# Blocks of a triangular inverse on the partitions in another order, with their transfers on other queues

## The chip, the core and the metric

The kernel runs on one core of a Trainium2 chip. The metric is device time in microseconds, the median of several executions. A core has five engines with a queue of instructions each, run in order: TensorE (PE in the profile, its weight loads PEld), VectorE (DVE), ScalarE (ACT), GpSimd (POOL) and SyncE (SP). SyncE computes nothing and issues transfers; ScalarE and GpSimd can issue transfers too. Transfers run on 16 DMA engines that all queues share.

## The reference, cut to what matters

One decoder layer on 512 tokens of width 1024: feed-forward, mixer, feed-forward, norm. The mixer has two branches. The change lies in the second, a gated delta rule with 16 value heads in 8 pairs (a pair shares its query and key head). For every chunk of tokens it needs the inverse `T` of a unit lower triangular matrix:

```python
A = jnp.where(strict, jnp.einsum('bhntk,bhnsk->bhnts', kb, k) * Lmat, 0.0)
T = lax.linalg.triangular_solve(eye + A, jnp.broadcast_to(eye, A.shape),
                                left_side=True, lower=True, unit_diagonal=True)
u = jnp.matmul(T, v * beta[..., None])
w = jnp.matmul(T, kb * jnp.exp(gam)[..., None])
```

Then a recurrence over the chunks uses the inverse. The kernel works with chunks of 128 tokens, so a head has four matrices of 128 x 128 and a pair has eight.

## The kernel before, in words

Dense products are made of weight slabs. `slab` loads 128 x 512 numbers into `raw` (three buffers, on SP's queue), ScalarE rounds them into `whi`, VectorE puts the rest into `wlo` (five buffers of each), and TensorE does three matmuls for every block (L101 to L103). A slab of four blocks is twelve matmuls of 512 columns; slabs for products laid out by tokens (`natural`, weights `wn`) feed matmuls of 256 columns instead.

The program first runs a feed-forward stage, then the mixer, then the second feed-forward stage. In the mixer the string `ORDER` lists steps in program order. `n` (g_n) builds the matrices of one pair and starts the inverse; `i` (g_inv) finishes it; `r` (g_rec) is one chunk of the recurrence, given a high priority; the rest (`q k v z t y`) are dense products that also serve as work beside the recurrences. From this program the framework builds one fixed order for each engine, by a timeline that it simulates at build time. So an edit in one place can move instructions of all engines.

Step `n` makes Gram products on TensorE (L589), loads two decay rows `gb` (gam_rows, L635), and forms `n2`, eight negated triangular matrices. Each has four diagonal blocks of 32 x 32, so a pair has 32 such blocks. They are inverted on GpSimd by substitution, with one column of the result after the other updated by rank-one steps; to spread this over 128 partitions, each block's 32 result columns are split into four groups of eight. The steps:

- `nb`: four stores (SP, L614) put the blocks into DRAM, by b, the place on the diagonal, and s, the matrix.
- `m` (called `gfs` in the profile): four loads bring all 32 blocks to 32 partitions each, once for each column group g. Partition is g, then b, then s (POOL, L617).
- `t` (`ft`): the start values, an identity, from a constant in DRAM (POOL, L619).
- 62 instructions on POOL, two for each of 31 columns (L623, L624).
- `nt`: one store of `t` into DRAM (POOL, L625).
- `tq` (`x` in the profile, from `nt`): sixteen loads of 8 KB, one for each b and g (SP, L629), which put block rows on the partitions.
- `tp`: VectorE copies `tq` into the right column order (L631).

Step `i` then transposes the blocks (VectorE, L658) and joins blocks of 32 to 64 and to 128 by matmuls (L669, L675). The output `yh` of the first branch's projection (y_h) is evicted by ScalarE (L766) and stored into `md` on ScalarE's queue (L767).

Of the kernel before, what the change touches and what calls it, by code (L numbers as in the profile page):

```python
# [8 lines left out]
F32 = mybir.dt.float32  # L9
# [7 lines left out]
P = 128  # L17
T = 512
NT = T // P
# [245 lines left out]
def mixer(tc, mp, e):  # L265
    nc = tc.nc
    pe, act, dve, pool, sp = nc.tensor, nc.scalar, nc.vector, nc.gpsimd, nc.sync
    cs, ident, tri, strict, hm, ones, mhalf = (e[k] for k in ("cs", "ident", "tri", "strict", "hm", "ones", "mhalf"))
    uh, ul, rbc, rcol, rhalf, h = (e[k] for k in ("uh", "ul", "rbc", "rcol", "rhalf", "h"))
    psc, dr, dense, slab, mm3, ux, hd, dbg = (  # L270
        e[k] for k in ("psc", "dr", "dense", "slab", "mm3", "ux", "hd", "dbg"))
    wt, wn, wab, wbh, wbg, wo, dta, psd = (e[k] for k in ("wt", "wn", "wab", "wbh", "wbg", "wo", "dtab", "psd"))

    def ps(name, lane="d"):
        return psc.tile([P, T], F32, tag="p" + lane, name=name, bufs=LANES[lane])

    def v3(ap, a):
        return ap.rearrange("p (a b) -> p a b", a=a)

    def bc(ap, n):  # L280

        return ap.unsqueeze(2).to_broadcast([ap.shape[0], ap.shape[1], n])
# [14 lines left out]
    for size, names in ((1024, "n2:2 gz:2 fs:1 ut:1"), (512, "kn:3 gm:1 qm:2 gb:2 ln:1 at:4 vb:4 t64:2 on:2"),  # L297
                        (256, "ft:1 tp:1 thg:2 x:1 we:1 s:3 w:1"), (128, "fm:1"), (64, "sm:3")):
        for it in names.split():
            n, b = it.split(":")  # L300
# [3 lines left out]
    eye4 = e["hmask"][:, 5:9].rearrange("p a (i c) -> p (a i) c", c=8)  # L304
# [56 lines left out]
    gtd = dr.tile([16, T], F32, name="gtd")  # L361
# [173 lines left out]
    md = dr.tile([KD, P, T], F32, name="md")  # L535
# [25 lines left out]
    def g_n(u, st):  # L561
        kq = st["kq"] = G["kq"][u % 4]
        kn = st["kn"] = G["kn"][u % 4]
        sm = st["sm"] = places["sm"]("sm", (P, 8, 8))
        for i in range(2):
            pt = ps("ptk", "e")
            for c in range(NT):
                pe.transpose(pt[:, c * P:(c + 1) * P], kq[:, c, i], ident)
            if i == 0:
                act.copy(kn, v3(pt, NT))  # L570
            for c in range(NT):
                pc = pt[:, c * P:(c + 1) * P]
                act.activation(pc, pc, AF.Square, accum_out=sm[:, 0, 4 * i + c:4 * i + c + 1])

        hs = slice(2 * u, 2 * u + 2)
        rk = sm[:, 1, 0:4]
        dve.tensor_scalar(rk, sm[:, 0, 0:4], 4.0 * EPS, None, op0=ALU.add)
        pool.tensor_tensor(rk, rk, mhalf[:, :4], op=ALU.pow)
        s8 = lambda i: v3(sm[:, i], NT)
        c2, c3, c1 = st["c2"], st["c3"], st["c1"] = s8(2), s8(3), s8(4)  # L580
        dve.scalar_tensor_tensor(c2, beta[:, :, hs], 1.0, bc(rk, 2), op0=ALU.mult, op1=ALU.mult)
        dve.scalar_tensor_tensor(c3, c2, -1.0, bc(rk, 2), op0=ALU.mult, op1=ALU.mult)
        dve.tensor_tensor(c1, c3, eg[:, :, hs], op=ALU.mult)
        dve.tensor_scalar(c2, c2, 0.5, None, op0=ALU.mult)
        gm, qm = places["gm"]("gm", (P, NT, P)), G["qm"]
        for hf in range(2):
            pq = ps("pgq", "e")
            for c in (2 * hf, 2 * hf + 1):
                pe.matmul(pq[:, (c % 2) * 256:(c % 2) * 256 + 256], kq[:, c, 0],  # L589
                          kq[:, c].rearrange("p a b -> p (a b)"), start=True, stop=True)  # L590
            p4 = pq.rearrange("p (c a b) -> p c a b", c=2, a=2)
            dve.tensor_tensor(gm[:, 2 * hf:2 * hf + 2], p4[:, :, 0], mid(strict, 2), op=ALU.mult)
            dve.tensor_tensor(qm[:, 2 * hf:2 * hf + 2], p4[:, :, 1], mid(tri, 2), op=ALU.mult)
        st["at"] = []
        n2 = st["n2"] = G["n2"][u % 2]
        for i in range(2):
            hd_ = 2 * u + i
            gb = gam_rows(hd_)

            a = G["at"][u % 4][i]  # L600
            for c in range(NT):
                act.activation(a[:, c], gb[:, c], AF.Abs, bias=gam[:, c, hd_:hd_ + 1], scale=-1.0)
            act.activation(a, a, AF.Exp, scale=-1.0)
            for c in range(NT):
                dve.scalar_tensor_tensor(n2[:, i, c], gm[:, c], c3[:, c, i:i + 1], a[:, c], op0=ALU.mult, op1=ALU.mult)
            dve.tensor_tensor(a, qm, a, op=ALU.mult)
            st["at"].append(a)


        nb = dr.tile([4, 8, 32, 32], F32, name=f"nb{u}")  # L610
        nt = dr.tile([4, 4, 8, 32, 8], F32, name=f"nt{u}")
        for b in range(4):
            r = slice(32 * b, 32 * b + 32)
            sp.dma_start(nb[b].rearrange("s i j -> i s j"), n2[r, :, :, r].rearrange("p a c j -> p (a c) j"))  # L614
        m = G["m"]
        for g in range(4):
            pool.dma_start(m[32 * g:32 * g + 32], nb.rearrange("b s i j -> (b s) i j"))  # L617
        t = places["ft"]("ft", (P, 32, 8))
        pool.dma_start(t, eye4)  # L619
        for j in range(31):  # L620
            n, w = 31 - j, j // 4 + 1
            tv = v3(places["fm"]("fm", (P, 96))[:, :n * w], n)
            pool.tensor_tensor(tv, bc(m[:, j + 1:, j], w), t[:, j:j + 1, :w].to_broadcast([P, n, w]), op=ALU.mult)  # L623
            pool.tensor_tensor(t[:, j + 1:, :w], t[:, j + 1:, :w], tv, op=ALU.add)  # L624
        pool.dma_start(nt.rearrange("g b s i c -> (g b s) i c"), t)  # L625
        tq = G["tq"]
        for b in range(4):
            for g in range(4):
                sp.dma_start(tq[32 * b:32 * b + 32, :, g], nt[g, b].rearrange("s i c -> i s c"))  # L629
        tp = st["tp"] = G["tp"][u % 2]  # L630
        dve.tensor_copy(tp.rearrange("p s (c g) -> p s c g", g=4), tq.rearrange("p s g c -> p s c g"))  # L631

    def gam_rows(hd_):
        gb = places["gb"]("gb", (P, NT, P))
        pool.dma_start(gb, gtd[hd_:hd_ + 1].rearrange("o (c b) -> o c b", c=NT).to_broadcast([P, NT, P]))  # L635
        return gb

    def g_v(j, st):
# [123 lines left out]
    def y_h(d):  # L762
        g = ta("yh")
        pt = dense(wbh[d], HH, lambda k: o_h[k])
        with tc.high_priority():
            act.copy(g, pt)  # L766
        act.dma_start(md[d], g)  # L767


    o_h = [None] * HH  # L770
    G = {"kq": [hv[:, i].rearrange("p (c a b) -> p c a b", c=NT, a=2) for i in range(3)]}
# [4 lines left out]
    ex = lambda i, *shape: op[i](f"x{i}", shape)  # L776
    tb, big, col = (P, NT, P), (P, 2, NT, P), (P, 256)

    def room():
        G["kn"] = [pl("kn", tb) for _ in range(3)]  # L780
        G["qm"] = pl("qm", tb)
        G["late"] = pl("qm", tb)
        G["n2"] = [pl("n2", big) for _ in range(2)]
        G["gz"] = [pl("gz", (P, NT, 256)) for _ in range(2)]
        G["at"] = [[pl("at", tb) for _ in range(2)] for _ in range(2)]
        G["vb"] = [[pl("vb", tb) for _ in range(2)] for _ in range(2)]
        G["ut"] = [pl("ut", (P, 8, P)), hv[:, 3].rearrange("p (s b) -> p s b", s=8)]
        G["t64"] = [pl("t64", (64, 8, 64)) for _ in range(2)]
        G["m"] = pl("fs", (P, 32, 32))
        G["tq"] = G["gz"][1].rearrange("p c (a b) -> p (c a b)", b=32).rearrange("p (s g c) -> p s g c", s=8, g=4)  # L790
        for n in ("x", "we", "w"):
            G[n] = [pl(n, col)]
        G["tp"] = [pl("tp", (P, 8, 32))]
        for z in (*G["ut"], *G["t64"]):
            pool.memset(z, 0.0)

    def more():
        G["kq"].append(ex(0, P, NT, 2, P))
        G["gz"].append(ex(1, P, NT, 256))
        for n, i in (("at", 2), ("vb", 3)):  # L800
            e_ = ex(i, *big)
            G[n].append([e_[:, 0], e_[:, 1]])
        e_ = ex(4, *big)
        G["kn"].append(e_[:, 0])
        G["at"].append([G["late"], e_[:, 1]])
        G["ut"].append(ex(5, P, 8, P))
        pool.memset(G["ut"][2], 0.0)
        G["tq"] = ex(6, P, 8, 4, 8)
        e_ = ex(7, P, 4, 256)
        for i, n in enumerate(("x", "we", "w")):  # L810
            G[n].append(e_[:, i])
        G["tp"].append(e_[:, 3].rearrange("p (a b) -> p a b", a=8))
# [33 lines left out]
    for i in range(VH):  # L846
        if i < 8:
            a, b = uh[:, i], ul[:, i]
        elif i < 14:
            ab = places[("n2", "n2", "gz", "gz", "fs", "ut")[i - 8]]("sop", (P, 2, T), F32R)  # L850
            a, b = ab[:, 0], ab[:, 1]
        else:
            a, b = (places[n]("so" + n, dt=F32R) for n in (("on", "on"), ("gm", "ln"))[i - 14])
# [6 lines left out]
    for d in range(8):  # L860
        mi, tg, g = (places[n]("m" + n) for n in ("kn", "vb", "at"))
# [4 lines left out]
        pt = dense(wbg[d], VH, lambda k: so[k], lane=MERGE[d])  # L866
# [5 lines left out]
        a, b = ab[:, 0], ab[:, 1]  # L872
# [3 lines left out]
    for d in range(8):  # L876
        hr = ta("hr")
        sp.dma_start(hr, hd[d])
        pt = dense(wo[d], KD, lambda k: ms[k])
# [21 lines left out]
def layout(i):  # L901
    f = {k: np.asarray(v) for k, v in i.items()}
# [8 lines left out]
    a = np.arange(P)  # L911
    sqc = np.stack([np.eye(P), a[:, None] <= a[None, :], a[None, :] < a[:, None]], 1)
    hmask = np.zeros((P, 9, 64))
    for l, hh in enumerate(LEVELS):
        g, b = np.divmod(np.arange(64), hh)
        hmask[:, l] = (a[:, None] >= 2 * hh * g) & (a[:, None] < 2 * hh * g + hh)
    eye4 = np.eye(32).reshape(32, 8, 4).transpose(2, 0, 1)
    hmask[:, 5:] = np.repeat(eye4, 32, axis=0).reshape(P, 4, 64)
    w_in = f["w_in"][0]
    off = np.cumsum([0, 1024, 1024, 1024, 1024, 1024, 1024, 2048, 16, 16, 2048, 1024, 1024])  # L920
    part = [w_in[:, off[j]:off[j + 1]] for j in range(12)]
# [34 lines left out]
```

## Time and profile before

| what | us |
|---|---|
| median of 3 runs | 1764.5 (1762.9 to 1766.72) |
| the profiled execution | 1758.87 |
| its span, first to last instruction | 1757.1 |
| TensorE busy | 1694.4 (96%) |
| VectorE, ScalarE, GpSimd busy | 954.5, 695.7, 340.6 |

The mean clock granted to TensorE is 0.983. The first feed-forward stage lasts until about 400 us, the pairs' inverses and recurrences lie between about 690 and 1270 us, the second feed-forward stage begins after 1350 us. In the profile a row of a timeline is start, duration, engine, line, operation, output and input; a bracket at its end tells how long the engine had been idle before it and whom it waited for. Rows of waits are: engine, instruction, what it waited for, then total time, count and longest. Tiles share buffers, and the profile names a buffer by one of its users, so `tq` and `tp` appear as `x` or `gtp`, the target of the transposes as `h`, `gut` or `x`.

### The profile page before, as it was taken

How to read it: one execution, taken by the hardware profiler on the slowest of the kernel's cores; microseconds unless marked ns; L12 is line 12 of the kernel's file. 1: busy time of each engine (PE TensorE's matmuls, PEld its weight loads, DVE VectorE, ACT ScalarE, POOL GpSimd, SP SyncE). 2: the span in 40 equal slices, each digit the busy share in tenths (PEclk: the TensorE clock that was granted, in tenths of full speed). 3: DMA queues.
4: the chain of work that ended last, by engine and by line, in shares of the span. 5: the costliest groups of instructions: out<-in, count | busy, mean ns of one | idle time of the engine just before them, and what ended most of it. 6: DMA issues, size and time to landing. Idle time of an engine off the chain costs nothing. (4 is left out here: it accounts for less than half of the span.)

```text
span 1757.1 us, 26109 instructions
## 1 busy us (share of the span) xinstructions
PE 1694.4 (96%) x9362; PEld 1430.0 (81%) x9362; DVE 954.5 (54%) x1968; ACT 695.7 (40%) x1525; POOL 340.6 (19%) x717
## 2 busy tenths in 40 slices
PE   7999999999999999899999999998899999999997
PEld 5888888889889997778878878886688888888886
DVE  4544443335675675455776776665564444444323
ACT  4433333332343334454454555444433433333332
POOL 2000000001121222770336435452000100000001
PEclk9999999999999999899999999998999999999998
DMA  4233233332221223442333343345463333323333
GB/s 154 90 96 96 97 95 110 112 116 66 73 75 53 61 84 115 144 123 55 106 102 100 100 114 93 104 117 156 144 186 114 109 98 99 97 96 93 99 94 108
DMA packets 141922, 182.17 MB, mean 104 GB/s; under 512 B 54992, under 2 KB 59600, under 8 KB 141792
## 3 DMA queue, kind: packets, MB, share of 16 engines
q1 hardware_dynamic: 132448, 159.52, 30.6%
q0 software_dynamic: 3584, 10.49, 2.1%
q10 hardware_dynamic: 5760, 10.49, 1.7%
q8 instruction: 74, 1.21, 0.3%
q14 instruction: 56, 0.46, 0.1%
HBM read 163.64 MB, written 16.81 MB: 103 GB/s over the span
## 5 line engine op out<-in xcount | busy, mean ns | idle before, releaser
L96 ACT CAST whi<-raw 128x512 fp32r<-128x512 f32 (+1 forms) x535 | 328.0, 614 | 643.0 <-PE pmm L102 541.3
L97 DVE TENSOR_TENSOR wlo<-raw,whi 128x512 fp32r<-128x512 f32 (+1 forms) x535 | 371.2, 695 | 368.0 <-ACT whi L96 365.1
L101 PE MATMUL pmm<-uh,whi 128*128 128x512 f32 x1288 | 514.3, 400 | 10.6 <-ACT whi L96 6.3
L102 PE MATMUL pmm<-ul,whi 128*128 128x512 f32 x1288 | 511.8, 397 | 1.9 <-DVE ul L128 1.7
L103 PE MATMUL pmm<-uh,wlo 128*128 128x512 f32 x1288 | 510.0, 396 | 0.0
L101 PEld LDWEIGHTS pmm<-uh,whi 128*128 128x128 f32 x1288 | 244.8, 190 | 63.3 <-ACT whi L96 6.5
L102 PEld LDWEIGHTS pmm<-ul,whi 128*128 128x128 f32 x1288 | 244.6, 190 | 55.3 <-DVE ul L128 6.0
L103 PEld LDWEIGHTS pmm<-uh,wlo 128*128 128x128 f32 x1288 | 244.3, 190 | 50.7 <-DVE wlo L97 0.2
L101 PE MATMUL pnat<-whi,uh 128*128 128x256 f32 x512 | 149.6, 294 | 1.1 <-DVE ggz L327 1.0
L102 PE MATMUL pnat<-wlo,uh 128*128 128x256 f32 x512 | 147.8, 290 | 0.0
L103 PE MATMUL pnat<-whi,ul 128*128 128x256 f32 x512 | 147.8, 290 | 0.0
L101 PE MATMUL pmm<-gh,whi 128*128 128x512 f32 (+1 forms) x374 | 141.0, 377 | 0.0
L103 PE MATMUL pmm<-gh,wlo 128*128 128x512 f32 (+1 forms) x374 | 140.9, 377 | 0.0
L102 PE MATMUL pmm<-gl,whi 128*128 128x512 f32 (+1 forms) x374 | 140.8, 377 | 0.0
L139 POOL TENSOR_TENSOR acc<-acc,sqt 128x512 f32<-128x512 f32 x24 | 32.7, 1363 | 526.3 <-ACT sqt L137 526.0
L101 PEld LDWEIGHTS pnat<-whi,uh 128*128 128x128 f32 x512 | 98.7, 193 | 2.8 <-DVE ggz L327 1.4
L102 PEld LDWEIGHTS pnat<-wlo,uh 128*128 128x128 f32 x512 | 99.0, 194 | 0.8
L623 POOL TENSOR_TENSOR fm<-gfs,ft 128x60 f32<-128x60 f32 (+24 forms) x248 | 91.3, 368 | 42.5 <-DMA gfs<-nb 17.8
L103 PEld LDWEIGHTS pnat<-whi,ul 128*128 128x128 f32 x512 | 98.5, 193 | 0.5
L624 POOL TENSOR_TENSOR ft<-ft,fm 128x60 f32<-128x60 f32 (+24 forms) x248 | 90.4, 365 | 18.9
L101 PEld LDWEIGHTS pmm<-gh,whi 128*128 128x128 f32 x374 | 70.4, 188 | 13.0
L103 PEld LDWEIGHTS pmm<-gh,wlo 128*128 128x128 f32 x374 | 70.4, 188 | 12.9
(345 smaller groups left out, 2115.7 us busy)
## 6 DMA issues: line engine op xcount, KB each, us to landing
raw<-wt SPq DMA_DIRECT2D x128, 256.0 KB, 2.8
raw<-w1a SPq DMA_DIRECT2D x88, 256.0 KB, 2.6
raw<-w1b SPq DMA_DIRECT2D x88, 256.0 KB, 2.6
raw<-wn SPq DMA_DIRECT2D x64, 256.0 KB, 3.1
raw<-w2b SPq DMA_DIRECT2D x45, 256.0 KB, 2.6
raw<-w2a SPq DMA_DIRECT2D x40, 256.0 KB, 2.6
raw<-wbg SPq DMA_DIRECT2D x32, 256.0 KB, 3.3
raw<-wbh SPq DMA_DIRECT2D x16, 256.0 KB, 2.8
```

Source lines behind the costliest of these rows:

```text
L96: act.copy(hi[:, :f], raw[:, :f])
L97: dve.tensor_tensor(lo[:, :f], raw[:, :f], hi[:, :f].bitcast(F32), op=ALU.subtract)
L101: pe.matmul(pt, ah, bh, start=first, stop=False)
L102: pe.matmul(pt, ah, bl, start=False, stop=False)
L103: pe.matmul(pt, al, bh, start=False, stop=last)
L139: pool.tensor_tensor(acc, acc, s, op=ALU.add)
L623: pool.tensor_tensor(tv, bc(m[:, j + 1:, j], w), t[:, j:j + 1, :w].to_broadcast([P, n, w]), op=ALU.mult)
L624: pool.tensor_tensor(t[:, j + 1:, :w], t[:, j + 1:, :w], tv, op=ALU.add)
```

## The change

The partition of a block is now b, then g, then s, instead of g, then b, then s. So each of the four `m` loads takes the eight blocks of one b and repeats them for the four groups, by a source with a leading dimension of four and step zero; and `tq` is loaded by four transfers of 32 KB, one for each b, instead of sixteen of 8 KB. The constant that holds the start values is reordered to match, and the copy into `tp` reads other strides. The `m` and `t` loads and the `nt` store move from GpSimd's queue to SP's; the decay rows `gb` move from GpSimd's queue to ScalarE's; the eviction of `yh` moves from ScalarE to VectorE and the store into `md` from ScalarE's queue to SP's. In the changed kernel the lines from the load of `t` (L619, then L620) to the store `nt` (L625, then L626) have a number higher by one; the others keep theirs.

```diff
-        nt = dr.tile([4, 4, 8, 32, 8], F32, name=f"nt{u}")
+        nt = dr.tile([4, 32, 32, 8], F32, name=f"nt{u}")
...
-        for g in range(4):
-            pool.dma_start(m[32 * g:32 * g + 32], nb.rearrange("b s i j -> (b s) i j"))
+        for b in range(4):
+            sp.dma_start(m[32 * b:32 * b + 32].rearrange("p i j -> p (i j)"),
+                         nb[b].rearrange("s i j -> s (i j)").unsqueeze(0).to_broadcast([4, 8, 1024]))
         t = places["ft"]("ft", (P, 32, 8))
-        pool.dma_start(t, eye4)
+        sp.dma_start(t, eye4)
...
-        pool.dma_start(nt.rearrange("g b s i c -> (g b s) i c"), t)
+        sp.dma_start(nt.rearrange("b q i c -> (b q) i c"), t)
         tq = G["tq"]
         for b in range(4):
-            for g in range(4):
-                sp.dma_start(tq[32 * b:32 * b + 32, :, g], nt[g, b].rearrange("s i c -> i s c"))
+            sp.dma_start(tq[32 * b:32 * b + 32], nt[b].rearrange("q i c -> i q c"))
         tp = st["tp"] = G["tp"][u % 2]
-        dve.tensor_copy(tp.rearrange("p s (c g) -> p s c g", g=4), tq.rearrange("p s g c -> p s c g"))
+        dve.tensor_copy(tp.rearrange("p s (c g) -> p s c g", g=4), tq.rearrange("p (g s) c -> p s c g", g=4))
...
-        pool.dma_start(gb, gtd[hd_:hd_ + 1].rearrange("o (c b) -> o c b", c=NT).to_broadcast([P, NT, P]))
+        act.dma_start(gb, gtd[hd_:hd_ + 1].rearrange("o (c b) -> o c b", c=NT).to_broadcast([P, NT, P]))
...
         with tc.high_priority():
-            act.copy(g, pt)
-        act.dma_start(md[d], g)
+            dve.tensor_copy(g, pt)
+        sp.dma_start(md[d], g)
...
-        G["tq"] = G["gz"][1].rearrange("p c (a b) -> p (c a b)", b=32).rearrange("p (s g c) -> p s g c", s=8, g=4)
+        G["tq"] = G["gz"][1].rearrange("p c (q b) -> p (c q) b", b=8)[:, :32]
...
-        G["tq"] = ex(6, P, 8, 4, 8)
+        G["tq"] = ex(6, P, 32, 8)
...
-    hmask[:, 5:] = np.repeat(eye4, 32, axis=0).reshape(P, 4, 64)
+    hmask[:, 5:] = np.tile(np.repeat(eye4, 8, axis=0), (4, 1, 1)).reshape(P, 4, 64)
```

## The prediction

> **What bounds the kernel now.** I read the page's busy table first, then stretches of time, then who waits on TensorE, then the path of one inverse in the timeline.
>
> ```profile
> PE 1694.4 (96%) x9362; PEld 1430.0 (81%) x9362; DVE 954.5 (54%) x1968; ACT 695.7 (40%) x1525; POOL 340.6 (19%) x717
> ...
> 100.00:125.00 25.00, 25.00 (x112) 20.68 (x112) 11.94 (x19) 8.61 (x15) 0.00 (x0) 1.00 0.32 102
> 675.00:1275.00 600.00, 562.11 (x3568) 472.41 (x3567) 374.61 (x854) 292.52 (x807) 245.66 (x609) 0.96 0.40 113
> 1200.00:1225.00 25.00, 18.30 (x145) 15.14 (x144) 14.53 (x39) 11.77 (x30) 1.66 (x1) 0.80 0.64 184
> 1225.00:1275.00 50.00, 43.62 (x219) 33.50 (x219) 27.50 (x74) 23.64 (x73) 3.27 (x2) 1.00 0.49 149
> ...
> PE pmm L101 <- ACT whi L96: 6.8, 2, 6.3
> PE pq L669 <- DVE h L658: 5.9, 4, 4.1
> PE pus L708 <- DVE x L705: 4.0, 3, 2.6
> PE pq L669 <- DVE gut L658: 2.4, 2, 2.2
> PE pq L675 <- ACT acc L671: 2.0, 1, 2.0
> ```
>
> In a stretch's row the columns are its length, then busy time with instruction counts of PE, PEld, DVE, ACT and POOL, then the granted clock, the DMA share and GB/s. TensorE is the bound: 112 wide matmuls fill 25 us of the first feed-forward stage, 0.223 us each (25 / 112). All that this change can touch lies between 675 and 1275 us, where TensorE is idle 600 - 562.1 = 37.9 us and has a mean clock of 0.96. Waits for the inverse itself (L669, L675) are 5.9 + 2.4 + 2.0 = 10.3 us of it; the other 27.6 us belong to the recurrences, the norms and the transposes. Missing weights are no problem: the wait on `whi` is 6.8 us in all, 6.3 of them one wait at the start.
>
> The path of one inverse, the last (pair 7), from the Gram matmuls (L589) to TensorE's first use (L669):
>
> ```profile
> 1150.02 1.02 PE L589 MATMUL pgq<-x 128*128 128x256 f32 x4
> ...
> 1159.70 1.87 SPq L614 DMA_DIRECT2D nb<-gn  x4
> 1163.30 1.96 POOL L617 DMA_DIRECT2D gfs<-nb  x4 [10.79 <-DMA nb<-gn]
> 1169.21 0.25 POOL L623 TENSOR_TENSOR fm<-gfs,ft 128x31 f32<-128x31 f32 x1 [3.96 <-DMA gfs<-nb]
> ...
> 1199.09 0.61 POOL L625 DMA_DIRECT2D nt<-ft  x1 [0.30 <-POOL ft L624]
> ...
> 1201.12 7.77 SPq L629 DMA_DIRECT2D x<-nt  x16
> 1210.50 0.39 DVE L631 COPY x<-x 128x256 f32<-128x256 f32 x1 [7.08 <-DMA x<-nt]
> 1211.86 0.31 PE L669 MATMUL pq<-h,gn 32*32 32x32 f32 x2 [4.06 <-DVE h L658]
> ...
> 976.85 1.10 PE L589 MATMUL pgq<-h 128*128 128x256 f32 x4 [1.15 <-DVE gqm L593]
> 1034.22 0.24 PE L669 MATMUL pq<-h,gn 32*32 32x32 f32 x2 [1.00 <-DVE h L658]
> ```
>
> The reader is to see that the path is as long as the work that was put beside it: 1211.86 - 1151.04 = 60.8 us in pair 7, 56.3 us in pair 4 (1034.22 - 977.95), and TensorE, which runs its queue in order, reaches L669 4.06 and 1.00 us too early. There is no slack worth the name. So what decides is a difference: how much shorter the path gets, against how much less work the changed order puts beside it.
>
> **What the new order takes away.** TensorE gets the same instructions in both kernels; only their order differs. I counted those between the last L589 and the first L669 of a pair in both orders, mean of pairs 2 to 7. Before: 128.3 matmuls of 512 columns, 103.3 of 256, 80.2 small ones. After: 99.7, 96.0 and 57.3. Priced at 0.223 us, half of that, and 0.13 us (the row below, 1.03 / 8), the loss is 28.6 x 0.223 + 7.3 x 0.112 + 22.9 x 0.13 = 6.4 + 0.8 + 3.0 = 10.2 us for each of six inverses. Pairs 0 and 1 lose about 5 and 7 us and I leave them out: pair 1 keeps 64 us of work beside its path, and pair 0 gains most at `tq`, as its sixteen issues were the slowest.
>
> ```profile
> 1268.27 1.03 PE L749 MATMUL pto<-sq,on 128*128 128x128 f32 x8
> ...
> 1208.99 1.34 SPq L94 DMA_DIRECT2D raw<-wbg  x3
> ...
> 1017.41 0.64 POOL L635 DMA_DIRECT2D gb<-gtd  x1 [0.26 <-ACT x L602]
> 1020.66 0.54 POOL L635 DMA_DIRECT2D gb<-gtd  x1
> ...
> q0 software_dynamic: 3584, 10.49, 2.1%
> ...
> raw<-w1a SPq DMA_DIRECT2D x88, 256.0 KB, 2.6
> ...
> x<-nt SPq DMA_DIRECT2D x128, 8.0 KB, 2.0
> ...
> nb<-gn SPq DMA_DIRECT2D x32, 32.0 KB, 1.7
> ```
>
> **What the path gains, step by step.**
> - *Loading `m`, other issue.* Each of the four loads needs one block `nb[b]` instead of all. The first can go some 0.3 + 1.7 = 2.0 us after the first store's issue (median landing 1.7) instead of 3.6 (1163.30 - 1159.70): 1.6 us gained. From the first issue to the loop took 5.9 us (1169.21 - 1163.30); on SP, with four issues at 0.47 (1.87 / 4) and a landing like a weight slab's 2.6, it would be 1.4 + 2.6 = 4.0: another 1.9. In all 3.5 us, if the transfer itself is as fast as before.
> - *Loading `m`, other shape.* It need not be. Before, each load reads 32 rows of 4 KB. After, the source is 8 rows repeated four times, an outer dimension of 4 with step zero. If a transfer is dealt to the 16 DMA engines along its outer dimension, this one has only four of them. The software queue, which carries these loads now, moved 10.49 MB in 2.1% of 16 engines' 1757.1 us: 590 engine-us, 17.8 GB/s per engine. Four loads of 131,072 bytes take 524,288 / (16 x 17.8) = 1.8 us on 16 engines and 7.4 us on four, 5.5 us more. No row shows a transfer of this shape, so the ends are a gain of 3.5 and a loss of 2.0. I take the loss: the row that gives the gain is for another shape, and the change puts the factor of four in front. On this term the Trainium skill speaks ("DMA: Bandwidth & Descriptors", Rules for kernel authors): the number of engines follows from the slowest dimension that is not of size 1, so a leading zero-step broadcast of c copies confines the whole transfer to at most c engines. By that rule this term is the loss of 2.0 us and the result the forecast; by the rows of the old shape it is the gain, and the result lies near the rival "even" below. No run so far shows which.
> - *The loop on POOL.* Two `gb` issues fall into some loops (0.64 + 0.54 us); they go to ScalarE's queue. 0 to 1.2 gained, 0.6 taken. The 62 instructions stay.
> - *`nt` on SP.* From POOL's issue to SP's first read took 2.0 us (1199.09 to 1201.12). From SP it should be the same; but SP must have reached it, and a weight slab ahead of it waits for up to 12 x 0.223 = 2.7 us. 0 to 2.7 lost, 0 taken: the wait table below has SP there early.
> - *`tq`: 4 loads for 16.* 16 issues took 7.77 us, 0.49 each for 256 pieces of 32 B; three slabs of 128 rows took 1.34, 0.45 each. Twice the pieces cost 0.04 more, so 1024 pieces cost some 0.49 + 6 x 0.04 = 0.73, the last of four issued 2.2 us after the first instead of 7.3. Landing may add 0.4. 4.7 us gained; the ends are 5.8 (pitch unchanged) and 0 (pitch proportional to pieces).
> - *`yh` and `md`.* Eight evictions leave ScalarE (579 ns below) for VectorE, 8 x 0.6 = 4.6 us between 718 and 759 us, and eight `md` issues of 0.33 go behind weight loads on SP. VectorE is 54% busy, SP's 96 saved `tq` issues are worth 43 us (96 x 0.449), so both are taken as nothing. With the cover gone they would cost those 4.6 us once.
> - *`gb` on ScalarE*: 16 issues at 0.33 like `md` now, 5.3 us on an engine that loses 8 x 0.58 + 8 x 0.33 = 7.2. Nothing. The reload of `t` stands right behind a pair's `tq` loads, well ahead of the next pair's `nb`: nothing.
>
> ```profile
> L766 ACT COPY yh<-pmm x8: 577/579/588, 718.3 to 753.7; 128x512 f32<-128x512 f32 x8
> L767 ACTq DMA_DIRECT2D md<-yh x8: 326/327/327, 718.9 to 758.9; - x8
> ...
> L629 SPq DMA_DIRECT2D x<-nt x128: 302/449/1431, 751.9 to 1208.4; - x128
> ...
> SPq L94 <- DVE wlo L97: 1113.8, 455, 17.9
> SPq L629 <- DMA nt<-ft: 31.9, 8, 9.3
> ```
>
> The path gets -2.0 + 0.6 + 0 + 4.7 = 3.3 us shorter, the cover 10.2 us. TensorE waits 6.9 us longer at each of six inverses: 41 us.
>
> **What of that reaches the end.** Not all. While TensorE waits at L669, VectorE and ScalarE catch up, and some of the 27.6 us of other waits vanish; I take half, -14. Slack at some L669 of around half a microsecond, six times: -3. A wait lowers the clock afterwards: in the slice with the 4.06 us wait it was 0.80, which costs 18.3 x 0.2 = 3.7 us; as some stretches are slow already, I add 1 us each, +6. The tail gains: pair 7's inverse stands some 12 us of work earlier, and its four recurrence steps, which stand within 13 us of work before, are spread over 26; the tail's idle is 6.7 + 6.4 = 13.1 us (the two last stretches above), of which I take 5 off. 41 - 14 - 3 + 6 - 5 = +25 us. The profiled execution took 1758.87 us (span 1757.1), the median of the runs is 1764.5, 5.6 above it; the 25 us are added to the median: 1789.5, say 1789.
>
> **The rivals.**
> - *Faster.* The `m` loads use all engines and the `tq` loads keep their pitch. Then the path gains 3.5 + 1.2 + 5.8 = 10.5 us, as much as the cover lost. TensorE's waits at L669 stay, the tail gives 5 us, and POOL, rid of `gb` issues that wait for buffers, may give 3 more around 700 us. -8: 1756. It decides once the path gains over 10.2. For it: the four DMA changes all shorten something that is on the path. Against it: both unknowns must fall at their best ends.
> - *Even.* All engines, but the middle price for `tq`: 3.5 + 0.6 + 4.7 = 8.8, so 1.4 us more at six inverses, 8 us, half of it absorbed, and 5 from the tail: 1764.
> - *Pieces.* All engines, but the `tq` loads go by pieces and save nothing: 4.1 gained, 6.1 lost at each, and 41 becomes 37: 1785.
> - *Weights starve.* SP waits in order for `nb`, for POOL's loop and for `nt`; behind it stand the slabs. Now it waits 31.9 us at `nt` in eight waits, 9.3 at most, and nothing starves, for five converted slabs cover 5 x 2.7 = 13.4 us. If the new waits last 16 us, TensorE loses 2.6 us eight times, 21 us on top: 1810. The sign would be waits of `pmm` on `whi` between 700 and 1210 us.
>
> **How the numbers follow.** The forecast (four engines) gets 0.55, with a range of its own from 1775 (28 us absorbed instead of 14: +11) to 1812 (nothing absorbed, and half of the 2.7 us lost at `nt` six times: 25 + 14 + 8 = +47). Weights starving 0.06, pieces 0.07, even 0.08, faster 0.24. That is 0.24 faster, 0.08 within 0.2% (3.5 us, about what a measurement of this kernel can tell from no change), 0.68 slower. The range 1755 to 1814 takes in all cases but about half of the faster one and the worst of starving.
>
> **What the changed profile would show.** Right: `gfs` loads on SP with landings well over 4 us, the last of the four latest, and 10 us or more from the first `nb` issue to the loop; L669 and L675 waits of 30 us or more instead of 10; a clock under 0.96 from 675 to 1275; `tq` four issues in under 3 us. Wrong: landings of `gfs` near 3 us (then even or faster), `tq` issues near 2 us each (pieces), or inverse waits that grow while the span does not, because other waits shrank by as much.

## The result and the profile after

The changed kernel takes 1793.32 us (median of 4 runs, 1789.26 to 1797.64), the kernel before 1764.10 us beside it: a ratio of 1.0164, 95% interval 1.0136 to 1.0192. It is 29 us slower. The execution that was profiled took 1797.64 us, 4.3 above its median, and that of before was 5.2 below its own median, so the two profiles lie 38.8 us apart where the medians lie 29 apart. Shares of the loss are what the profiles can give, not its last microseconds.

The stretch with the inverses in the changed kernel (a row has the length, then busy time and count of PE, PEld, DVE, ACT and POOL, then granted clock, DMA share and GB/s):

```profile
675.00:1275.00 600.00, 538.36 (x3394) 450.92 (x3393) 353.93 (x802) 267.75 (x746) 201.66 (x544) 0.94 0.37 104
```

The answering row of before had 562.11 us of TensorE and a clock of 0.96. So the idle time of TensorE in these 600 us went from 37.9 to 61.6, +23.7 us. The price of the lower clock is better summed over short stretches: over 48 of 12.5 us each, busy time x (1 - granted clock) comes to 20.9 us before and 30.0 after, +9.1. Together +32.8 us of the 38.7 between the two spans (1795.8 - 1757.1). Before 675 us the same sum is 3.3 us apart, behind 1275 us 1.6 us. Most of the 3.3 is one stretch of low clock at the start (0.50 from 17 to 24 us), which nine of the other kernels of this case show as well, far ahead of the changed lines. The change lost its time where the inverses are.

One inverse of the changed kernel, that of pair 2, in the timeline:

```profile
864.71 1.81 SPq L614 DMA_DIRECT2D nb<-gn  x4
866.57 3.27 SPq L617 DMA_DIRECT2D gfs<-nb  x4
...
875.33 0.26 POOL L624 TENSOR_TENSOR fm<-gfs,ft 128x31 f32<-128x31 f32 x1 [14.55 <-DMA gfs<-nb]
...
905.63 3.97 SPq L629 DMA_DIRECT2D x<-nt  x4
...
911.71 0.40 DVE L631 COPY gtp<-x 128x256 f32<-128x256 f32 x1 [0.73 <-DMA x<-nt]
...
914.77 0.69 PE L669 MATMUL pq<-x,gn 32*32 32x32 f32 x32
```

The four loads of `m` are issued by 869.84 and POOL's loop starts at 875.33, 10.6 us after the first `nb` store; the four `tq` loads take 3.97 us to issue. And TensorE reaches L669 with no wait at all, 2.7 us after the copy. That is the surprise of this profile, and the table of who TensorE waited for repeats it:

```profile
PE pto L749 <- DVE on L745: 9.6, 6, 3.4
PE pto L749 <- ACT x L724: 6.4, 1, 6.4
PE pmm L101 <- ACT whi L96: 6.2, 2, 5.7
...
PE pq L669 <- ACT gut L678: 4.3, 1, 4.3
PE pto L749 <- DVE s L714: 4.1, 1, 4.1
PE pmm L101 <- DVE yh L766: 4.0, 1, 4.0
...
PE pq L669 <- DVE x L658: 1.5, 2, 1.3
...
PE pq L669 <- DVE h L658: 0.5, 2, 0.3
PE pq L669 <- DVE gut L658: 0.4, 2, 0.3
...
PE pq L675 <- ACT acc L671: 0.2, 1, 0.2
```

The inverse's own first matmuls (L669, L675) waited 10.3 us before and wait 6.9 now. What grew most is L749, the transposes of a recurrence step's normed output: 20.1 us, against these two rows in the kernel before:

```profile
PE pto L749 <- ACT x L724: 1.8, 1, 1.8
PE pto L749 <- DVE on L745: 0.6, 2, 0.4
```

So this one line waits 17.7 us more, where all idle time together grew by 23.7; other lines changed both ways. Where these waits come from is seen in the largest of them, rows of the changed kernel's timeline and then of its stretches:

```profile
962.14 1.65 POOL L740 TENSOR_TENSOR sm<-sm,mhalf 128x8 f32<-128x8 f32 x1
963.75 0.29 POOL L624 TENSOR_TENSOR fm<-gfs,ft 128x54 f32<-128x54 f32 x1
963.82 0.25 DVE L741 TENSOR_TENSOR sm<-sm,rcol 128x8 f32<-128x8 f32 x1 [7.18 <-POOL sm L740]
...
964.60 0.76 ACT L602 ACTIVATE gat<-gb,gx 128x128 f32<-128x128 f32 x2 [5.97 <-DVE on L745]
965.27 0.41 ACT L724 COPY x<-pog 128x128 f32<-128x128 f32 x2
965.73 1.11 PE L749 MATMUL pto<-sq,on 128*128 128x128 f32 x4 [6.42 <-ACT x L724]
```
```profile
960.00:964.00 4.00, 0.00 (x0) 0.00 (x0) 0.18 (x1) 0.00 (x0) 3.61 (x8) 0.82 0.01 2
964.00:966.00 2.00, 0.27 (x2) 0.27 (x2) 1.96 (x7) 1.40 (x6) 1.53 (x7) 0.50 0.00 0
966.00:968.00 2.00, 2.00 (x7) 1.52 (x7) 2.00 (x8) 2.00 (x6) 1.53 (x7) 0.50 0.17 58
968.00:970.00 2.00, 2.00 (x7) 1.56 (x7) 0.65 (x3) 1.29 (x5) 1.30 (x6) 0.66 0.56 203
```

POOL runs its queue in order, and the power of the norm (L740) stands between two steps of the loop of the inverse. The loop started late, so L740 came late, and VectorE sat 7.18 us at L741. ScalarE then waited 5.97 us for VectorE's next line (L745); behind that wait in its queue stood the copy L724, which TensorE's row names, and TensorE sat 6.42 us at L749. From 964 to 968 us the granted clock is 0.50 and then 0.66 for 2 us more, so TensorE works at half speed right after the wait. Over the whole run VectorE's waits on this one operation went from 12.2 to 31.8 us, the row of before first:

```profile
DVE sm L741 <- POOL sm L740: 12.2, 3, 5.8
```
```profile
DVE sm L741 <- POOL sm L740: 31.8, 5, 7.6
```

The steps of the path, each read from the timelines (mean of pairs 2 to 7, us). "Work beside" is TensorE's work between the last L589 and the first L669, counted in its order and priced with durations of the profile of before; the last two rows are runs of the next section. The path and its steps are measured, the work beside it is worked out.

| kernel | first `nb` issue to loop | loop | loop end to first `tq` issue | first `tq` issue to copy | path, `nb` to end of copy | work beside | path - work |
|---|---|---|---|---|---|---|---|
| before | 9.36 | 28.96 | 2.93 | 10.26 | 51.9 | 55.0 | -3.1 |
| after | 11.49 | 27.63 | 2.08 | 6.08 | 47.7 | 44.6 | +3.1 |
| eight engines (below) | 9.25 | 27.68 | 2.11 | 5.76 | 45.2 | 44.6 | +0.6 |
| one load (below) | 7.77 | 28.10 | 1.79 | 6.61 | 44.7 | 44.1 | +0.6 |

### The profile page after: what moved, and what is told of

Same layout as the page of the kernel before. It is cut to its first block, busy times and chain, and to the rows that moved or that the text cites. A ratio compares the mean times of both kernels' runs of the same rounds, so it can differ in the third digit from the quotient of the medians.

```text
span 1795.8 us, 25951 instructions
## 1 busy us (share of the span) xinstructions
PE 1708.1 (95%) x9362; PEld 1438.7 (80%) x9362; DVE 955.4 (53%) x1976; ACT 690.1 (38%) x1517; POOL 299.6 (17%) x653
## 5 line engine op out<-in xcount | busy, mean ns | idle before, releaser
L139 POOL TENSOR_TENSOR acc<-acc,sqt 128x512 f32<-128x512 f32 x24 | 32.8, 1367 | 526.0 <-ACT sqt L137 525.6
L625 POOL TENSOR_TENSOR ft<-ft,fm 128x60 f32<-128x60 f32 (+24 forms) x248 | 88.5, 357 | 19.1
L548 DVE SCALAR_TENSOR_TENSOR cy<-ci,cs,cy 128x512 f32<-128x512 f32 x96 | 74.1, 772 | 21.5 <-ACT cy L546 20.6
L102 PEld LDWEIGHTS pmm<-gl,whi 128*128 128x128 f32 x374 | 70.4, 188 | 13.0
```

Of the source, the lines that this page charges most:

```text
L102: pe.matmul(pt, ah, bl, start=False, stop=False)
L139: pool.tensor_tensor(acc, acc, s, op=ALU.add)
L548: dve.scalar_tensor_tensor(y, ci[:, j:j + T], wc[j], y, op0=ALU.mult, op1=ALU.add)
```

## The experiments

The theory after the result: each inverse is later against the work planned beside it, as the last column says, and one part of this is the shape of the `m` loads. Rivals: the small operations on POOL between the steps of the loop are the actual cause; the new places of the waits on SP cost the time, whatever the path; the other order by itself costs it.

**The same issues, another shape of the `m` loads.** The repetition goes inside, so that the source's slowest dimension is 8 instead of 4. The rows of the inverse change places with it, which the mask and the copy to `tp` answer for. Every engine's order of instructions stays that of the changed kernel.

```diff
             sp.dma_start(m[32 * b:32 * b + 32].rearrange("p i j -> p (i j)"),
-                         nb[b].rearrange("s i j -> s (i j)").unsqueeze(0).to_broadcast([4, 8, 1024]))
+                         nb[b].rearrange("s i j -> s (i j)").unsqueeze(1).to_broadcast([8, 4, 1024]))
...
-        dve.tensor_copy(tp..., tq.rearrange("p (g s) c -> p s c g", g=4))
+        dve.tensor_copy(tp..., tq.rearrange("p (s g) c -> p s c g", g=4))
...
-    hmask[:, 5:] = np.tile(np.repeat(eye4, 8, axis=0), (4, 1, 1)).reshape(P, 4, 64)
+    hmask[:, 5:] = np.tile(eye4, (32, 1, 1)).reshape(P, 4, 64)
```

> The four loads of m take the same blocks, but the repetition by four is the inner dimension (partition b, s, g) and the outer one has 8; constant and copy are reordered to match. All engines have the very same order of instructions as in the changed kernel, so only the loads can act. Theory (a load is dealt to the DMA engines along its outer dimension, and the late loop on GpSimd makes the rest late): the four loads take 3.7 us instead of 7.4, the loop starts 6 to 9 us after the first nb issue instead of 9.5 to 12.3, and the time falls from 1793 to between 1772 and 1782. Rival (the loads do not matter, the loss is that the new order has 10 us less work beside each inverse): the loop starts as late as before, time 1789 to 1797.

Measured: 1781.27 us, a ratio of 1.0098 (1.0081 to 1.0115), where the changed kernel has 1.0164 (1.0136 to 1.0192). The difference is 0.0066 x 1764 = 11.6 us. The time lies in the range of the theory; the loop starts 9.25 us after the first `nb` issue, which is earlier than the 11.49 of the changed kernel and still later than the 6 to 9 expected. Pair 2 of this run, and the stretch:

```profile
862.87 3.67 SPq L617 DMA_DIRECT2D gfs<-nb  x4
...
869.34 0.37 POOL L624 TENSOR_TENSOR fm<-gfs,ft 128x31 f32<-128x31 f32 x1 [12.18 <-DMA gfs<-nb]
```
```profile
675.00:1275.00 600.00, 551.81 (x3477) 463.56 (x3475) 367.01 (x833) 276.52 (x765) 203.39 (x545) 0.94 0.38 108
```

From the first issue to the loop took 6.5 us here (869.34 - 862.87) and 8.8 in the changed kernel (875.33 - 866.57), with issues that took no less. TensorE's busy time in the stretch is 13.4 us higher (551.81 - 538.36). The two kernels have the same instructions in the same order on every engine, and the reordered copy into `tp` takes 0.41 us against 0.39, so it is shown that the shape costs the changed kernel about 12 us: a path 2.5 us shorter at six inverses, 15 us, against 12 that come back. The waits at L749 go with it, from 20.1 to 13.9 us. Now the DMA share while these loads run, first in the changed kernel, then in this one:

```profile
869.00:870.00 1.00, 1.00 (x5) 0.82 (x6) 0.58 (x1) 0.58 (x2) 0.00 (x0) 1.00 0.23 66
870.00:871.00 1.00, 1.00 (x6) 0.83 (x5) 1.00 (x3) 0.63 (x1) 0.00 (x0) 1.00 0.22 86
...
872.00:873.00 1.00, 1.00 (x6) 0.84 (x5) 0.41 (x1) 0.56 (x1) 0.00 (x0) 1.00 0.93 272
```
```profile
864.00:865.00 1.00, 1.00 (x16) 0.89 (x16) 0.12 (x1) 0.74 (x2) 0.00 (x0) 1.00 0.41 90
865.00:866.00 1.00, 1.00 (x9) 0.80 (x7) 0.28 (x1) 0.88 (x2) 0.00 (x0) 1.00 0.45 152
```

In the changed kernel the share stands at 0.22 and 0.23 of 16 engines, close to what four busy engines give (0.25), although the last of the four loads is issued by 869.84; when the weight slabs come through it is 0.93. With eight rows outermost it reaches 0.41 and 0.45, under the 0.50 of eight engines. The Trainium skill ("DMA: Bandwidth & Descriptors", Rules for kernel authors) says that a leading broadcast of c copies confines a transfer to at most c engines; these shares agree with it. The events that the trace records when transfers land agree too, and they are exact counts: every transfer of the kernel before leaves 16 on its semaphore, an `m` load of the changed kernel leaves 5, one with eight rows outermost 9, and the single load of the next run 16 again. From four rows to eight, four more events come in. The profile prints no landing times for these two kernels, but the last event of each load gives them: from issue to landing the four loads of a pair take 3.8, 4.7, 5.3 and 6.7 us in the changed kernel (medians, first to fourth) and 2.9, 3.2, 3.7 and 4.3 with eight rows outermost. The weight slabs behind them suffer too: of 133 slabs between 675 and 1275 us, 19 in the changed kernel have the last four of their 16 events over 0.8 us behind the others, and none with eight rows outermost or in the kernel before. How much of the 12 us goes through these slabs, and how much through the path, is not told apart.

**One load of all blocks.** The same reordering, but a single load whose slowest dimension is 32.

```diff
-        for b in range(4):
-            sp.dma_start(m[32 * b:32 * b + 32].rearrange("p i j -> p (i j)"),
-                         nb[b].rearrange("s i j -> s (i j)").unsqueeze(0).to_broadcast([4, 8, 1024]))
+        sp.dma_start(m.rearrange("p i j -> p (i j)"),
+                     nb.rearrange("b s i j -> (b s) (i j)").unsqueeze(1).to_broadcast([32, 4, 1024]))
```

> One load of 512 KB for all 128 partitions, outer dimension 32, repetition by four inside; it waits for all four nb stores. The order of instructions is planned anew. Theory: 1.9 us of transfer, loop start 6 to 7 us after the first nb issue, time 1755 to 1770. Rival (less cover): an order as tight as that of the changed kernel, time 1785 or more. Rival (SP's queue): SP waits for the stores before the load, weights come late, 1785 or more with TensorE waits on whi.

Measured: 1769.27 us, 1.0035 (1.0021 to 1.0048): 12 us faster than the last run, 6.5 slower than before. The time is in the theory's range; the loop starts 7.77 us after the first `nb` issue, where 6 to 7 were expected.

```profile
862.80 0.53 SPq L616 DMA_DIRECT2D gfs<-nb  x1
...
867.91 0.26 POOL L623 TENSOR_TENSOR fm<-gfs,ft 128x31 f32<-128x31 f32 x1 [13.40 <-DMA gfs<-nb]
```
```profile
675.00:1275.00 600.00, 553.13 (x3525) 465.18 (x3524) 370.57 (x846) 282.33 (x787) 204.58 (x545) 0.96 0.38 110
```

The load's issue to the loop is 5.1 us, and the clock is back at 0.96: the sum over short stretches gives 18.9 us for the clock, 46.9 of idle. Against the eight-engine run idle time is nearly the same (48.2), the clock's part 6.5 us less (25.4). Two things changed at once here, the shape and the number of issues, and TensorE's order with them; these 12 us are therefore not split further. Path minus work is the same +0.6 in both, so that difference alone does not tell the time.

**The queues alone, and the layout alone.** First the kernel before with its old blocks and all moves between queues:

```diff
-            pool.dma_start(m[32 * g:32 * g + 32], nb.rearrange("b s i j -> (b s) i j"))
+            sp.dma_start(m[32 * g:32 * g + 32], nb.rearrange("b s i j -> (b s) i j"))
...
-        pool.dma_start(t, eye4)
+        sp.dma_start(t, eye4)
-        pool.dma_start(nt.rearrange("g b s i c -> (g b s) i c"), t)
+        sp.dma_start(nt.rearrange("g b s i c -> (g b s) i c"), t)
-        pool.dma_start(gb, ...)
+        act.dma_start(gb, ...)
-            act.copy(g, pt)
-        act.dma_start(md[d], g)
+            dve.tensor_copy(g, pt)
+        sp.dma_start(md[d], g)
```

> The kernel before with all its moves of queues (m, t, nt on SP, gb on ScalarE, yh on VectorE, md on SP), but the old order of blocks: m in four loads of 32 rows without a repetition, tq in 16 loads. Theory: loads on all engines, the loop starts 7 us or less after the first nb issue (8.2 to 9.5 before), time 1755 to 1768. Rival (SP's queue is what costs): 1785 or more, although no load is confined.

Then the changed kernel's blocks, with `m`, `t`, `nt` and `gb` left on POOL's queue and `yh`, `md` as they were:

```diff
-            pool.dma_start(m[32 * g:32 * g + 32], nb.rearrange("b s i j -> (b s) i j"))
+            pool.dma_start(m[32 * b:32 * b + 32].rearrange("p i j -> p (i j)"),
+                         nb[b].rearrange("s i j -> s (i j)").unsqueeze(0).to_broadcast([4, 8, 1024]))
...
-                sp.dma_start(tq[32 * b:32 * b + 32, :, g], nt[g, b].rearrange("s i c -> i s c"))
+            sp.dma_start(tq[32 * b:32 * b + 32], nt[b].rearrange("q i c -> i q c"))
```

> The new order of blocks with the repeated source, but m, t, nt and gb on GpSimd's queue and yh, md as before. Theory, if the repeated source confines a transfer on this queue too: loop start 11 us or more after the first nb issue, time 1780 to 1800. If only SP's queue deals by the outer dimension: loop start near 8 us, time 1755 to 1768. Rival (SP's queue is what costs): 1755 to 1768 as well, with loads of normal speed.

Measured: 1771.91 us, 1.0044 (1.0029 to 1.0059), and 1770.59 us, 1.0035 (1.0022 to 1.0047). Some 8 and 6 us, where the whole change costs 29. Neither theory came out: the loop starts 8.40 and 9.46 us after the first `nb` issue, where 7 or less and, for the second, 11 or more or near 8 were expected, and both times lie between the ranges. In the `m` loads the one has the old shape on SP, the other the new shape on POOL's queue:

```profile
L617 SPq DMA_DIRECT2D gfs<-nb x32: 312/419/425, 713.2 to 1178.5; - x32
...
DMA to landing us min/median/max: 2.1/2.7/4.1
```
```profile
L617 POOL DMA_DIRECT2D gfs<-nb x32: 572/588/658, 711.1 to 1180.4; - x32
...
DMA to landing us min/median/max: 3.5/4.8/6.7
```

On SP the old shape is issued in 0.42 us and lands in 2.7 us; before, on POOL's queue, it landed in 3.5. On POOL's queue the new shape lands in 4.8. So either half of the change holds something that would shorten the path (2.5 us of path in the first, 4.4 in the second), and both are slower than the kernel before. That the halves do not add up to the whole speaks for the pair: from the first `nb` issue to the loop the new shape takes 3.1 us more than the old one on SP (11.49 against 8.40) and 0.1 more on POOL's queue (9.46 against 9.36). That the path is not all is what these two runs add. With the queues alone TensorE has one wait of 9.7 us, as much as this kernel loses, and it comes from SP's queue:

```profile
780.31 0.33 SPq L625 DMA_DIRECT2D nt<-ft  x1
...
784.35 0.62 ACT L96 CAST whi<-raw 128x512 fp32r<-128x512 f32 x1 [7.20 <-DMA raw<-wn]
...
785.65 1.06 PE L675 MATMUL pq<-acc,gtp 32*32 32x32 f32 x32 [9.74 <-ACT acc L671]
```

SP issued its last slab before this at 766.62 us, then stood at `nt` until POOL's loop ended, and loaded the next slab (`raw<-wn`) only after 780.31. ScalarE waited 7.20 us for that slab, and the copy L671 that TensorE needed stood behind it. So the rival "SP's queue" is real, though not in the size expected.

**The small operations taken off POOL.** The table of waits names L740 and L542 (the zero columns in front of a convolution) as what everyone waits for. If POOL's order is the cause, the loss should go with them. The power is taken as an estimate from the bits and three Newton steps on VectorE.

```diff
-        pool.memset(ci[:, :3], 0.0)
+        dve.memset(ci[:, :3], 0.0)
...
-        pool.tensor_tensor(rho, rho, mhalf[:, :8], op=ALU.pow)
+        dve.tensor_scalar(y_.bitcast(I32), rho.bitcast(I32), 1, None, op0=ALU.logical_shift_right)
+        dve.tensor_scalar(y_.bitcast(I32), y_.bitcast(I32), -1.0, float(0x5f3759df), op0=ALU.mult, op1=ALU.add)
+        for _ in range(3):
+            dve.tensor_tensor(t_, y_, y_, op=ALU.mult)
+            dve.scalar_tensor_tensor(t_, t_, -0.5, rho, op0=ALU.mult, op1=ALU.mult)
+            dve.scalar_tensor_tensor(y_, t_, 1.5, y_, op0=ALU.add, op1=ALU.mult)
+        dve.tensor_copy(rho, y_)
```

> The changed kernel with the small operations that stand amid the inverse's loop on GpSimd taken off it: the zeroing of ci (L542) and the power -1/2 of the recurrence's norm (L740) go to VectorE, the power as a bit estimate with three Newton steps, 12 small instructions. The loads of m stay confined. Theory (the late loop acts through these operations: 40 us of VectorE's and 20 us of ScalarE's waits on GpSimd): these waits vanish, the loop still starts 9.5 us or more after the first nb issue, and the time falls from 1793 to 1765 to 1780, although the cover beside an inverse is no longer (42 us of work). Rival (the late inverse acts at L669 itself, and the small operations are a symptom): waits at L669 and L631 take their place, 1788 or more.

The same two moves in the kernel before, as a control:

> The same two moves in the kernel before, where the waits on GpSimd are 17 us. Theory: a small gain, 1750 to 1762, because less of these waits reaches TensorE there. Rival (the planned order with less cover, 50 us for 55, costs more than the waits): 1766 to 1776.

The same in the kernel with one load:

> Both remedies on the changed kernel: one load of m for all partitions, and the small operations off GpSimd. Theory: the shortest path with nothing behind the loop, 1748 to 1762, below the kernel before. Rival (cover of 43 us is too little for any path): 1766 or more, with waits at L669 of over 15 us.

And the zero columns alone, the first of the two edits:

> The changed kernel with only the zeroing of ci on VectorE; the power stays amid the loop. ScalarE waits 20 us and VectorE 8 us for it in the changed kernel. Theory: these waits vanish, those for the power (32 us) stay, 1780 to 1790. Rival (symptom only): 1790 or more.

Measured: 1797.57 us, 1.0207 (1.0185 to 1.0228), for the changed kernel with both moves; 1777.47 us, 1.0092 (1.0060 to 1.0123), for the control; 1783.63 us, 1.0132 (1.0106 to 1.0158), for one load with both; 1797.80 us, 1.0213 (1.0190 to 1.0235), for the zero columns alone. None is faster than the kernel it was made from; the theories' ranges were missed in all four, and the three changed kernels came out in the ranges of the rivals, the control just above that of its own. The control shows that the moves by themselves cost some 16 us. TensorE's waits with both moves on the changed kernel:

```profile
PE pq L669 <- DVE h L658: 19.2, 4, 7.7
PE pq L669 <- DVE gut L658: 16.9, 4, 8.6
PE pq L669 <- DVE x L658: 16.3, 4, 9.4
```

and with the zero columns alone:

```profile
PE pto L749 <- DVE on L745: 15.2, 5, 4.0
PE pq L669 <- DVE h L658: 9.1, 4, 7.8
PE pq L669 <- DVE gut L658: 8.0, 1, 8.0
```

With both operations off POOL the waits at L749 are down from 20.1 to 1.1 us (that line is L757 there), and L669 waits 52.4 us instead of 6.7. With one of them gone the wait is split between the two places. The idle time of the stretch from 675 to 1275 us is 65.2 and 65.4 us, where the changed kernel has 61.6. So the small operations are mainly where the lateness shows, not where it comes from: TensorE meets it at the first thing in its order that hangs on the late inverse, by POOL's order or by the data. As the whole cause this rival fell. A share of it is not excluded: with the operations off POOL the change costs 1.0207 / 1.0092, some 20 us, and with them on POOL 29, and each of these kernels also has an order of its own.

**More work beside the inverse.** What is left of the loss with one load, 6.5 us, might be missing work beside the path. The list by which the planner starts inverses and feed-forward groups was written anew, with later inverses of the later pairs; the first entries of the part that changes:

```diff
-    "G3 S3 O6 O7 R0 q1 k1 q0 k0 t0 t1 t2 t3 y0 y1 y2 y3 y4 y5 y6 y7 R1 n0 n1 i0 q2 k2 v0 v1 z0 r0 r0 "
-    "v2 v3 n2 z1 q3 k3 i1 t4 r0 r1 r0 i2 r1 v4 v5 z2 n3 r0 q4 k4 t5 v6 v7 z3 r1 r2 r1 i3 r2 n4 r1 "
+    "R1 n0 n1 q2 k2 v0 v1 z0 i0 r0 r0 v2 v3 n2 z1 q3 k3 t4 r0 i1 r1 r0 r1 v4 v5 z2 n3 "
+    "r0 q4 k4 i2 t5 v6 v7 z3 r1 r2 r1 r2 n4 r1 q5 k5 t6 v8 v9 i3 z4 r2 r3 r2 r3 n5 r2 "
```

> The changed kernel with one m load (as in the run with one load) and the list that starts the inverses and the feed-forward groups rewritten: the inverses of later pairs start up to eight entries later against the groups. By the same pricing of TensorE's order the work beside an inverse is 47.2 us in the mean of pairs 2 to 7, against 44.1 with the old list; nearly all of it comes from pair 3 (60.7 against 44.2). Theory (too little work beside the path is what is left): pair 3's late inverse goes, 3 to 4 us faster than the one load's 1769, so 1765. Rival (what is left is the new place of the waits on SP and POOL, not the cover): 1769 or more.

> The kernel before with the same rewritten list, a control: its work beside an inverse is 52.9 us against 55.0 with its own list. Theory: that is about its path (51.5), so it stays or loses a few us: 1762 to 1770. If the list by itself were better, it would be faster than before, and the gain of the other run would not be due to the cover.

Measured: 1767.98 us, 1.0049 (1.0031 to 1.0066), for one load with the new list; 1769.42 us, 1.0049 (1.0030 to 1.0068), for the kernel before with it. Two rows of TensorE's waits in the first:

```profile
PE pq L668 <- DVE x L657: 4.2, 1, 4.2
PE pq L668 <- DVE h L657: 4.2, 4, 2.7
```

In the first the path is 43.4 us and the work beside it 47.2: a margin of 3.8 us, more than the 3.1 of before. The waits of the inverse's first matmuls for the transposes are 8.4 us, before's 8.3, and it is still no faster than with the old list (1.0035). So missing work in the mean is not what is left; this theory missed by its own number, 1765. The control is 8.6 us slower than before with nothing changed but the list. With this list the old transfers and the new ones with one load come out at the same ratio.

Five kernels, then, stand 0.35 to 0.49% above before: the queues alone, the layout alone, one load, and the new list with either set of transfers. All have another order of TensorE's work than the kernel before. For the queues alone one wait, of 9.7 us, is as large as the loss; in the other four no single wait does, and which property of the old order is worth their 6 to 9 us stays open. Of the 29 us of the change 12 are shown to belong to the four-engine loads, against eight engines; some 11 to 12 more went with a single load instead of four on eight engines, of which shape, issues and order are not told apart; and the last 6 us are that remainder. No kernel here beats the kernel before. A version with the old order of TensorE and the new transfers was not tried, since the planner makes the order from the program.

## Why the prediction was right

The forecast was 1789 us, slower with a chance of 0.68, and 1793.3 us came. The deciding difference, path against work, and the confined loads were right. That the number came so close is partly luck: at the front end two sizes cancelled, at the far end the place of the wait and what became of the other waits were wrong, and the sum of 25 us was worked out from a profile, while the two profiled spans lie 38.7 us apart.

- *The difference that decides.* The path was to get 3.3 us shorter and the work beside it 10.2. From the timelines the path is 51.9 - 47.7 = 4.2 us shorter; priced by the order with the durations used here, the work is 55.0 - 44.6 = 10.4 less. So 6.2 us at each of six inverses, 37 us, where 41 stood in the sum.
- *Loading `m`.* The sum of the two terms was a loss of 2.0 us, and it is 11.49 - 9.36 = 2.1. But neither term was right. The other issue was to gain 3.5, of which 1.9 stood for the move to SP: with the old shape on SP the step takes 8.40 us (queues alone, mean of pairs 2 to 7), a gain of 1.0. The other 1.6, for needing one block instead of all, no run isolates. The other shape was to cost 5.5: between four and eight engines the same step differs by 11.49 - 9.25 = 2.2, and to one load on all engines, with three issues fewer besides, by 3.7. The sign "10 us or more from the first `nb` issue" came (10.6 to 12.3 in these pairs); so did that of the landings, well over 4 us with the last the latest (5.1 us in the median, 6.7 for the fourth). The new loads also take longer to issue, 612 ns in the median against 419 of the old shape on SP; the prediction had taken 470.
- *The loop on POOL.* 0.6 us were taken from a range of 0 to 1.2; it got 1.3 us shorter.
- *`nt` on SP.* Nothing was taken, with up to 2.7 lost. From the loop's end to the first `tq` issue it is 2.93 before and 2.08 now, 0.85 gained. SP was there early, as said: it waits 75.6 us for POOL at this place.

```profile
SPq L626 <- POOL ft L625: 75.6, 7, 22.0
```

- *`tq`.* 4.7 us were to be gained by a pitch of 0.73 us. From the first issue to the copy it is 4.2 less. The pitch is 0.84 us (the four issues take 3.36 in the mean of these pairs), so the sign "four issues in under 3 us" came only at its edge, in two pairs of the six.
- *`yh` to VectorE.* Taken as nothing, 4.6 us if its cover was gone. TensorE's table has one wait of 4.0 us on `yh` (L766), but not for the price of the eviction, which takes 0.68 us. It stood in VectorE's queue behind two slabs that came late, and with eight rows outermost this wait is 0.5 us:

```profile
758.19 0.62 ACT L96 CAST whi<-raw 128x512 fp32r<-128x512 f32 x1 [12.24 <-DMA raw<-wt]
...
762.31 0.68 DVE L766 COPY yh<-pmm 128x512 f32<-128x512 f32 x1
```

- *Where the wait stands.* "L669 and L675 waits of 30 us or more" is a sign that failed: 6.9 us. The step behind it took L669 for the first instruction in TensorE's order that a late inverse holds up. POOL's and VectorE's orders have other instructions between the steps of the loop, and TensorE comes to those first. The kernel with the small operations off POOL shows the wait at the place predicted, 52.4 us at L669. That this is near 41 + 10.3 is chance in part: 16.3 us of it stand in pairs 0 and 1, which the prediction left out, and the order of that kernel is its own.
- *What of it reaches the end.* 41 - 14 - 3 = 24 us of idle time were forecast beside the tail, and 23.7 came in the stretch from 675 to 1275 us. The step between is wrong all the same: the other waits, 27.6 us before, were to shrink by 14 while TensorE sat at L669; in place of that the inverse's waits shrank to 6.9 us and all others grew to 54.7. The clock was to cost 6 and cost 9.1; the sign of a mean clock under 0.96 came (0.94). The tail was to gain 5 us: its idle time was 13.1 us before (1200 to 1275 us) and is 10.6 now (1230 to 1315 us), so half of that came. With the tail in, 19 us of idle time were forecast, and 24.3 came behind 675 us.
- *The rivals.* "Weights starve" had SP waits of 16 us in it; they reached 22.0 us, and yet TensorE's wait on `whi` is 6.2 us, 5.7 of it one wait, where before had 6.8. The starving came once and under another name, in the 4.0 us at `yh` above. SP had stood 9.1 us at `nt` until 748.27 us and issued the four `m` loads before the next slab (751.86); that slab had 12 of its 16 events by 756.00 and the last four only at 757.88 to 758.09, after the last `m` load had landed (757.33). ScalarE waited 12.24 us for it. The sign named for this rival, waits of `pmm` on `whi`, does not show it. "Pieces" had its sign in part (a pitch of 0.84 us, not near 2). "Faster" needed 10.5 us of path; with all engines and one load 7.2 came (51.9 - 44.7), and that kernel is not faster either.

## What to carry to other kernels

Read a change to a path that runs beside other work as a difference: how much shorter the path gets and how much less work the new order puts beside it. Here it gave the direction and, as 37 us against 24 us of new idle time, the order of magnitude; it did not rank kernels that lie close, for two with the same difference (+0.6) were 12 us apart. Look at the slowest dimension of a load, also where it is a repetition: four copies outermost held the DMA share near a quarter, and eight rows outermost, with all else the same, were 12 us faster. Do not take the instruction at which an engine waits for the cause of the wait: moving those operations away sent the wait to the next place, and a late slab showed as a wait for an eviction. Keep a control for the new order itself: a rewritten list alone cost this tuned kernel 8.6 us.

## What the runs showed of the hardware beside this

- Of two `m` loads with the same 32 rows of 4 KB, the one whose source repeats took longer to issue. On SP the old load took 419 ns in the median; the new one with four copies outermost took 612, with the copies inside 655 (row not shown). On POOL's queue it was 492 and 588. One load of all blocks took 525 ns on SP for four times the bytes.

- After TensorE's wait of 6.42 us the granted clock was 0.50 for 4 us and 0.66 in the mean of the next 2; TensorE's busy time x (1 - clock) from 964 to 970 us is 0.27 x 0.5 + 2 x 0.5 + 2 x 0.34 = 1.8 us, over a quarter of the wait itself.
